# A fixed order for a kernel's first loads, and four weight copies moved from the opening into the half products

## The chip, the cores and the metric

The kernel runs on one core of one Trainium2 chip. The metric is the device time of one execution in microseconds; the median of the runs shown is compared. A core has a matrix engine (TensorE, here PE, with its weight loads as PEld), VectorE (DVE), ScalarE (ACT), GpSimd (POOL), and SyncE (SP), which here only issues transfers. Transfers are issued on the queue of SP, ACT or POOL and carried out by 16 DMA engines that all of them share.

## The reference

One inference step of a one-layer hybrid encoder in float32: 1024 prompt frames and 64 sample frames (1088 in all), model width 1024.

```
xn = rms_norm(x, g_pre)
z  = xn @ w_in                 # one projection, columns cut into
                               # xa, ga | q, k, v, gb | fl (16 columns) | ma, mb
ua = causal_conv(xa, width 4);  ya = rg_lru(ua) * silu(ga)
logf = log_sigmoid(fl + b_f)    # per head and frame
yb = softmax(q k / 8 + sum of logf between key and query, causal) v * silu(gb)
mix = (sigmoid(ma) * (ya @ w_branch[0]) + sigmoid(mb) * (yb @ w_branch[1])) @ w_o
h  = x + rms_norm(mix, g_post)
y  = h + rms_norm(sigmoid(h @ w_ple_gate) * (p @ w_ple_proj), g_ple)
```

Returned are y, the keys k, the values v, logf and the last states of branch A, for prompt and sample.

## The kernel before

**Arithmetic.** A product that must be as exact as float32 is made of three passes: each operand is split into a high part (a rounded copy made by ACT, names ending in `h`) and a low part (the difference, made by DVE, names ending in `l`), and PE adds high x high, low x high and high x low.

**Stages.** (1) The opening, 0 to some 35 us: the first two blocks of 128 frames (`x_in`) are normalised, transposed and split, while the V columns of `w_in` arrive as eight weight rows of 128 x 1024 numbers (`load_wv(k)`, k = 0 to 7, 512 KB each) and are split into `wvh` and `wvl`. Rows 0 to 2 and 5 to 7 share three buffers `wv_raw`, so row 5 can be loaded when row 0 is split, and so on; rows 3 and 4 lie in the two halves of `w_raw`. PE takes up each row for both blocks as soon as it is split (`rows(b, [k], VC)`, 6 matmuls of 346 columns each); the last 348 columns hold 16 for the forget logits too, which come from the small load `wf_raw` (128 x 8 pieces of 64 bytes). (2) The V projection of the other blocks to about 101 us, then two panels of a gate. (3) The half products: twelve passes of `seven` (from about 152 to 415 us), each of which gives two 128-column panels of k, q or a gate from seven products of half size. A pass has its raw weights loaded two passes ahead (`load_pair`, alternately into `w_raw` and `wraw`) and split one pass ahead. Keys are turned (`tpk`) and copied by ACT to a staging tile (`st`, two buffers, or `kst`, one), from which SP's queue stores them into the output (`keys_out`). `tpk`, `cum_p` and `ct` share one PSUM tag with two buffers. (4) Attention, the recurrence of branch A, the branch projections, the output projection with `w_o`, and the last normalisations.

**The copies of `w_o`.** `copy_weights(n)` copies one 512 x 512 quarter of `w_o` (1 MB) inside DRAM into `d_w`, laid out so that the output projection, after 1000 us, can load it in one piece. In the source its four calls stand in the recurrence of branch A.

**What sets the order.** PE's order is the written one; ACT and DVE keep the written order in marked stretches (`manual_schedule`), the opening among them. Everything else is placed by a scheduler, which keeps an instruction at its written place only where it is passed through `tc.keep_in_program_order`. SP executes its transfers in the order that the scheduler gives: an issue that has to wait holds up all that follow. Each transfer reports to one of eight completion counters (`DMAHW0` to `DMAHW7`), given out in turn over SP's and ACT's queues together; a transfer whose counter was last used by one that hasn't landed is not issued until that one has, and the issuing engine stands meanwhile.

Of the kernel before, what the change touches and what calls it, by code (L numbers as in the profile page):

```python
# [13 lines left out]
P = 128  # L14
D = 1024
KT = D // P
# [5 lines left out]
NH = 16  # L22
# [5 lines left out]
C_XA, C_GA, C_Q, C_K, C_V, C_GB, C_FL, C_MA, C_MB = (  # L28
    0, 1024, 2048, 3072, 4096, 5120, 6144, 6160, 7184)
# [36 lines left out]
def hybrid_step(tc, a, o):  # L66
    nc = tc.nc
    PSUM = bass.MemoryType.PSUM
    act, dve, pool, pe, sp = nc.scalar, nc.vector, nc.gpsimd, nc.tensor, nc.sync
# [8 lines left out]
    def f(ap):  # L78
        return ap.bitcast(F32)

    def copy_act(out, in_, scale=1.0):
        return act.activation(out=out, in_=in_, func=AF.Copy, scale=scale)  # L82

    def sub(eng, out, in0, in1):
        return eng.tensor_tensor(out=out, in0=in0, in1=in1, op=ALU.subtract)  # L85
# [16 lines left out]
    NW = D // 2  # L102
    d_w = dram.tile([4, P, 4 * NW], F32, name="d_w")

    def copy_weights(n):

        i, j = n // 2, n % 2
        sp.dma_start(d_w[n].rearrange("p (k n) -> p k n", k=4),
                     a["w_o"][i * NW:(i + 1) * NW, j * NW:(j + 1) * NW].rearrange("(k p) n -> p k n", p=P))


    cst = sb("cst")
# [87 lines left out]
    def run(steps):  # L200
        for _ in steps:
            pass

    def chunk(steps):
        for _ in range(KT):
            next(steps)

    w_in = a["w_in"]
# [11 lines left out]
    def panels(src):  # L220
        return [src[..., i * P:(i + 1) * P] for i in range(2)]
# [99 lines left out]
    lp = flp.tile([P, NH], F32, name="lp")  # L321
    bf = p1.tile([P, NH], F32, name="bf")
# [4 lines left out]
    wf_raw = p1.tile([P, KT, NH], F32, name="wf_raw")  # L327
    xsl = p1.tile([P, KT, P], F32R, name="xsl")
    p1x = sb("p1x")
    g_pre = p1x.tile([P, D], F32, name="g_pre")  # L330
# [4 lines left out]
    def load_x(b):  # L335
        src, n, _ = x_src[b]
        t = p1x.tile([P, D], F32, name="x_in", tag="x_in", bufs=2)
        sp.dma_start(t[:n, :], src)
        x_in.append(t)

    raws = {}

    def load_wv(k):
        if k in (3, 4):
            raw = raw_half[k - 3]
        else:
            raw = p1x.tile([P, D], F32, name="wv_raw", tag="wv_raw", bufs=3)
        sp.dma_start(raw[:, :], w_in[k * P:(k + 1) * P, C_V:C_V + D])
        raws[k] = raw

    def split_wv(k):
        raw = raws.pop(k)
        copy_act(wvh[:, k, :D], raw[:, :])
        sub(dve, wvl[:, k, :D], raw[:, :], f(wvh[:, k, :D]))
# [67 lines left out]
    def turn_diag(b):  # L422
        x, dg = x_in[b], turned[b]
        turned[b] = [p1t.tile([P, 4, P], F32, name="tp", tag="tp") for _ in range(2)]
        for k in range(KT):
            pe.matmul(turned[b][k // 4][:, k % 4, :], x[:, k * P:(k + 1) * P], dg[:, :], start=True, stop=True)

    def x_hi(b, ks):
        for k in ks:
            copy_act(xs[k][0][:, b * P:(b + 1) * P], turned[b][k // 4][:, k % 4, :], scale=gT[:, k:k + 1])  # L430
# [8 lines left out]
    gT = p1.tile([P, KT], F32, name="gT")  # L439
    load_x(0)  # L440
    act.dma_start(g8[:, :], a["g_pre"].rearrange("(k p) -> k p", p=P))
    load_wv(0)
    load_x(1)
    for k in range(1, KT):
        load_wv(k)
        if k == 4:
            sp.dma_start(wf_raw[:, :, :], w_in[:, C_FL:C_FL + NH].rearrange("(k p) n -> p k n", p=P))
    wake = p1t.tile([P, 512], F32, name="wake", tag="tp")
    g_p = mm.tile([P, 512], F32, name="g_p", tag="acc")
    for i in range(WAKE):  # L450
# [4 lines left out]
    def weights(k, c):  # L455
        c0, w = VCH[c]
        return wvh[:, k, c0:c0 + w], wvl[:, k, c0:c0 + w]
# [6 lines left out]
    def rows(b, ks, cs=(0, 1, 2)):  # L464
        for k in ks:
            xh, xl = (t[:, b * P:(b + 1) * P] for t in xs[k])
            for p in (0, 2, 1):
                for c in cs:
                    w = VCH[c][1]
                    wh, wl = weights(k, c)  # L470
                    pe.matmul(pair[b][c][:, :w], xl if p == 2 else xh, wl if p == 1 else wh,  # L471
                              start=(k == 0 and p == 0), stop=(k == KT - 1 and p == 1))
# [6 lines left out]
    turn_diag(0)  # L479
    second = rstd_diag(1)  # L480
    split_wv(0)
    next(second)
    x_hi(0, [0])
    x_lo(0, [0])
# [2 lines left out]
    rows(0, [0], VC)  # L487
    run(second)
    split_wv(1)
    rows(0, [1], VC)  # L490
    turn_diag(1)
    for ks in (range(2, 4), range(4, KT)):
        x_hi(0, ks)
        x_lo(0, ks)
    split_wv(2)
    x_hi(1, (0, 1))
    x_lo(1, (0, 1))
    rows(0, [2], VC)
    rows(1, (0, 1), VC)
    x_hi(1, range(2, KT))  # L500
    x_lo(1, range(2, KT))
    sp.dma_start(g_pre[:, :], a["g_pre"].partition_broadcast(P))
    load_x(2)
    load_x(3)
    act.dma_start(bf[:, :], a["b_f"].partition_broadcast(P))
    sp.dma_start(lp[:, :], a["cache_logf"])

    vec = p1.tile([96, P], F32, name="vec")
    at = 0
    for name in ("conv_w", "conv_b", "b_rg_a", "b_rg_x", "a_param", "state_h", "state_conv"):  # L510
        n = a[name].shape[0]
        sp.dma_start(vec[at:at + n, :], a[name])
        at += n
    V_CW, V_CB, V_BA, V_BX, V_AP, V_H0, V_HIST = 0, 32, 40, 48, 56, 64, 72
    pool.memset(fl[:, NBLK, :], 0.0)
# [66 lines left out]
    for b in range(2, NBLK + 1):  # L582
        _, n, t0 = x_src[b]
# [50 lines left out]
    def load_pair(i):  # L634
        raw = sp_.tile([P, KT, 2 * P], F32, name="wraw", tag="wraw", bufs=1)[:, :, :] if i % 2 else raw_pair
        src = quads[i][0]
        for dst, s in zip([raw] if len(src) == 1 else panels(raw), src):
            load_panel(dst, s)
        return panels(raw)

    def split_pair(i, raws_, got):

        a1, a2 = raws_
        a11, a12, a21, a22 = a1[:, :4, :], a1[:, 4:, :], a2[:, :4, :], a2[:, 4:, :]

# [24 lines left out]
        split(sp_, ("s4",), [s4], 1)  # L670
        yield
# [239 lines left out]
    for i in range(len(quads)):  # L911
        nxt, w_nxt = None, {}
        last = i + 1 == len(quads)
        if not last:
            if i + 2 < len(quads):
                pairs.append(load_pair(i + 2))
            nxt = split_pair(i + 1, pairs[i + 1], w_nxt)
        else:
            held_back[0] = False
            look_ahead()  # L920
        seven(i, w, nxt, last)
        w = w_nxt
# [323 lines left out]
    for u, (h, q2) in enumerate(units):  # L1246
        p = h // 2
# [85 lines left out]
    while s_q or t_q or v_q:  # L1333
# [156 lines left out]
    def state(k):  # L1490
        state_in(k)
        scan(k)
# [61 lines left out]
    split_u(0)  # L1554
    run(xa)
    for k in range(0, KT - 2, 2):
        for n in range(k, min(k + 2, 4)):
            copy_weights(n)
        ga = own_gate(k)
        if k == 0:  # L1560
            chunk(ga)
        gate(k)
        convolve(k + 1)
        mix_u(k)
        if k:
            early_gate(k - 1)
        if k:
            split_y(k - 2)
            chunk(ga)
        split_u(k + 1)  # L1570
        chunk(ga)
        if k:
            state(k - 1)
            output(k - 1)
        run(ga)
        own_gate(k + 1)
        xa = recur_in(k + 2)
# [99 lines left out]
    for of in range(KT):  # L1677
# [16 lines left out]
        if of == 2:  # L1694
# [4 lines left out]
            at = 0  # L1699
# [368 lines left out]
    for k in range(2):  # L2068
        raw = p7.tile([P, D], F32, name="ple")
# [67 lines left out]
    n = x_src[b][1]  # L2137
# [68 lines left out]
```

## Time and profile before

| | us |
|---|---|
| median of 3 runs | 1464.6 |
| lowest, highest | 1464.26, 1467.74 |
| the profiled execution, its time | 1467.15 |
| the profiled execution, its span | 1465.4 |
| PE busy in the span | 1436.0 |
| granted TensorE clock, mean | 0.994 |

The span runs from the first to the last instruction of the one execution that was profiled; 1.75 us of its time lie around it. PE stands still for 29.4 us in the span, and for 2.24 us of that at one place in the opening. In a row of the timeline stand the start, the length, the engine (a name ending in q is the engine's issue of a transfer), the line, the operation, what it writes and reads, the count, and in brackets how long the engine had stood before it and on whom it had waited. A table of stretches gives for each engine its busy time and number of instructions, then the granted clock (1.00 is full speed), the mean share in which the 16 DMA engines were busy, and GB/s.

### The profile page before, as it was taken

The numbers are of one execution on the slowest core, as the hardware profiler recorded it, in microseconds if no ns is written. First come the engines' busy times: TensorE is split into PE (matmuls) and PEld (weight loads), VectorE is DVE, ScalarE is ACT, GpSimd is POOL, SyncE is SP. The second block draws the span as 40 slices with busy tenths as digits, with TensorE's granted clock in tenths as the row PEclk, the third lists the DMA queues.
The fourth block names the chain that finished last, engine by engine and source line by source line (L and its number), as shares of the span: only waits on it lengthen the run. The fifth ranks groups of instructions, "written<-read, shape, count | busy, mean of one in ns | idle before, by whom it ended". The sixth has DMA issues, their size and how long they took to land.

```text
span 1465.4 us, 25652 instructions
## 1 busy us (share of the span) xinstructions
PE 1436.0 (98%) x9653; PEld 1394.7 (95%) x9653; DVE 893.7 (61%) x1631; ACT 717.1 (49%) x1353; POOL 299.1 (20%) x385
## 2 busy tenths in 40 slices
PE   8999999999999999999999999999999999999997
PEld 8999999999999999999899989999999999879997
DVE  5464866564325666666466555898755574778534
ACT  4423444442215566666456556777444232554633
POOL 0013324323123332333233210221023000000001
PEclk9999999999999999999999999999999999999999
DMA  8457456754276565646545344454278774224111
GB/s 285 143 119 109 130 163 189 181 178 127 78 210 157 120 148 139 141 112 139 118 129 128 61 108 70 86 101 84 99 235 273 257 218 152 100 86 171 43 43 44
DMA packets 149304, 200.64 MB, mean 137 GB/s; under 512 B 24212, under 2 KB 115836, under 8 KB 148156
## 3 DMA queue, kind: packets, MB, share of 16 engines
q1 hardware_dynamic: 129772, 167.06, 44.2%
q10 hardware_dynamic: 17680, 25.64, 5.1%
q0 software_dynamic: 1728, 6.29, 2.3%
q8 instruction: 76, 1.25, 0.4%
q14 instruction: 48, 0.39, 0.1%
HBM read 131.04 MB, written 65.80 MB: 134 GB/s over the span
## 4 chain that ended last, share of the span: by engine, by line
PE 84%; DVE 7%; ACT 4%; DMA 3%; issue 2%; SPq 0%; POOL 0%; ACTq 0%; DVEq 0%; POOLq 0%
PE quad L805 17%; PE acc L170 12%; PE acc L172 12%; PE acc L171 12%; PE q L1853 5%; PE tp L1147 4%; PE pv L1175 2%; PE s L1125 2%; PE s L1126 2%; PE pv L1177 2%; PE vacc L170 1%; PE vacc L171 1%; PE vacc L172 1%; PE vacc L471 1%; PE q L1978 1%
## 5 line engine op out<-in xcount | busy, mean ns | idle before, releaser
L170 PE MATMUL acc<-xh,wh 128*128 128x364 f32 (+1 forms) x768 | 253.2, 330 | 1.3 <-ACT st L82 1.2
L171 PE MATMUL acc<-xl,wh 128*128 128x364 f32 (+1 forms) x768 | 252.0, 328 | 0.0
L172 PE MATMUL acc<-xh,wl 128*128 128x364 f32 (+1 forms) x768 | 251.8, 328 | 0.0
L170 PEld LDWEIGHTS acc<-xh,wh 128*128 128x128 f32 x768 | 144.9, 189 | 2.6 <-ACT st L82 1.9
L171 PEld LDWEIGHTS acc<-xl,wh 128*128 128x128 f32 x768 | 144.7, 188 | 0.5
L172 PEld LDWEIGHTS acc<-xh,wl 128*128 128x128 f32 x768 | 144.5, 188 | 0.0
L1105 DVE CUSTOM_DVE_ANT_0 s<-s,mask 128x1024 f32<-128x1024 f32 (+7 forms) x128 | 95.5, 767 | 26.8 <-PE s L1126 26.7
L85 DVE TENSOR_TENSOR wl<-w_raw,wh 128x1024 fp32r<-128x1024 f32 (+1 forms) x54 | 62.6, 1160 | 67.3 <-ACT wh L82 66.3
L1110 POOL TENSOR_SCALAR pb<-pb,sm 128x896 f32<-128x896 f32 (+1 forms) x64 | 61.8, 966 | 196.2 <-DVE sm L1109 178.2
L82 ACT ACTIVATE wh<-w_raw 128x1024 fp32r<-128x1024 f32 (+1 forms) x66 | 64.3, 976 | 65.6 <-PE quad L805 27.3
L85 DVE TENSOR_TENSOR tl<-tp,th 128x512 fp32r<-128x512 f32 x96 | 65.7, 688 | 35.6 <-ACT th L82 35.6
L805 PE MATMUL quad<-xh,wh 128*128 128x272 f32 x384 | 80.7, 291 | 0.0
L805 PE MATMUL quad<-xl,wh 128*128 128x272 f32 x384 | 79.5, 288 | 0.0
L805 PE MATMUL quad<-xh,wl 128*128 128x272 f32 x384 | 79.4, 288 | 0.0
L82 ACT ACTIVATE th<-tp 128x512 fp32r<-128x512 f32 x96 | 56.9, 596 | 40.6 <-PE tp L1147 33.4
L1107 ACT ACTIVATE pb<-s,nm 128x896 f32<-128x896 f32 (+1 forms) x64 | 61.1, 954 | 30.0 <-DVE nm L1105 27.7
L1125 PE MATMUL s<-k,q 128*128 128x256 f32 (+1 forms) x192 | 67.1, 353 | 0.2 <-ACT pb L1107 0.2
L1147 PE MATMUL tp<-ident,pb 128*128 128x128 f32 x416 | 63.9, 274 | 1.2 <-DVE diag0l L85 0.7
L1126 PE MATMUL s<-k,q 68*128 68x256 f32 (+1 forms) x192 | 65.0, 350 | 0.0
L171 PE MATMUL acc<-ybl,wh 128*128 128x364 f32 (+1 forms) x192 | 62.9, 328 | 0.0
L172 PE MATMUL acc<-ybh,wl 128*128 128x364 f32 (+1 forms) x192 | 62.8, 327 | 0.0
L170 PE MATMUL acc<-ybh,wh 128*128 128x364 f32 (+1 forms) x192 | 62.7, 326 | 0.0
(705 smaller groups left out, 4151.8 us busy)
## 6 DMA issues: line engine op xcount, KB each, us to landing
w_raw<-in_w_in SPq DMA_DIRECT2D x56, 256.0 KB
q<-d_q SPq DMA_DIRECT2D x48, 256.0 KB
k<-d_k SPq DMA_DIRECT2D x48, 256.0 KB
w_raw<-in_w_in SPq DMA_DIRECT2D x64, 128.0 KB
w_raw<-in_w_branch SPq DMA_DIRECT2D x32, 256.0 KB
wl<-w_raw POOLq DMA_DIRECT2D x12, 512.0 KB, 4.6
wraw<-in_w_in SPq DMA_DIRECT2D x20, 256.0 KB
d_k<-oh ACTq DMA_DIRECT2D x16, 272.0 KB
```

What stands on the lines that cost most here:

```text
L82: return act.activation(out=out, in_=in_, func=AF.Copy, scale=scale)
L85: return eng.tensor_tensor(out=out, in0=in0, in1=in1, op=ALU.subtract)
L170: pe.matmul(out, ah, bh, start=start, stop=False)
L171: pe.matmul(out, ah, bl, start=False, stop=False)
L172: pe.matmul(out, al, bh, start=False, stop=stop)
L805: pe.matmul(acc[:, c, :CW], l[:, k, :], r[:, k, c * CW:(c + 1) * CW], start=(first and k == 0 and p == 0), stop=(k == 3 and p == 2), skip_ ...
L1105: at = book("D", now[0] + HOP_PE, per(D_MAX, n), lambda: dve.tensor_tensor_reduce(out=s[:, :n], in0=s[:, :n], in1=m, scale=-1.0, scalar=-N ...
L1110: return free, book("G", at, per(G_NORM, n), lambda: pool.tensor_scalar(out=pr[:, :n], in0=pr[:, :n], scalar1=sm, scalar2=1.0, op0=ALU.mul ...
L1125: pe.matmul(s[:, c0:c0 + w], t["q1"][:, q0:q0 + P], t["k1"][:, c0:c0 + w], start=True, stop=False)
L1126: pe.matmul(s[:, c0:c0 + w], t["q2"][:HD + 4, q0:q0 + P], t["k2"][:HD + 4, c0:c0 + w], start=False, stop=True)
L1147: pe.transpose(tp[:, o0 + i * P:o0 + (i + 1) * P], pr[par][:, kb * P:(kb + 1) * P], ident[:, :])
L1853: pe.matmul(acc, l[:, k, :], r[:, k, :], start=(first and k == 0 and i == 0), stop=(k == 3 and i == 2), skip_group_check=not first)
```

## The change

All loads of the opening are fixed in the order in which they are written (`fetch`), and that order is: the two blocks of `x` and rows 0 to 4; rows 5, 6 and 7 after the splits of rows 0, 1 and 2; then the third block of `x`, `wf_raw`, `g_pre`, the fourth block, and the small vectors. `b_f`'s load, which ACT issues, stands right behind the load of `g8`. The four copies of `w_o` are taken out of branch A and written, fixed in place, into passes 0 to 3 of the half products, each behind that pass's `load_pair`.

```diff
     def copy_weights(n):
         i, j = n // 2, n % 2
-        sp.dma_start(d_w[n]..., a["w_o"][...])
+        tc.keep_in_program_order(sp.dma_start(d_w[n]..., a["w_o"][...]))
...
     def load_x(b):
...
-        sp.dma_start(t[:n, :], src)
+        fetch(t[:n, :], src)
...
+    def fetch(dst, src):
+        tc.keep_in_program_order(sp.dma_start(dst, src))
...
     def load_wv(k):
...
-        sp.dma_start(raw[:, :], w_in[k * P:(k + 1) * P, C_V:C_V + D])
+        fetch(raw[:, :], w_in[k * P:(k + 1) * P, C_V:C_V + D])
...
     load_x(0)
     act.dma_start(g8[:, :], a["g_pre"].rearrange("(k p) -> k p", p=P))
+    act.dma_start(bf[:, :], a["b_f"].partition_broadcast(P))
     load_wv(0)
     load_x(1)
-    for k in range(1, KT):
+    for k in range(1, 5):
         load_wv(k)
-        if k == 4:
-            sp.dma_start(wf_raw[:, :, :], ...)
...
     split_wv(0)
+    load_wv(5)
...
     split_wv(1)
+    load_wv(6)
...
     split_wv(2)
+    load_wv(7)
...
-    sp.dma_start(g_pre[:, :], a["g_pre"].partition_broadcast(P))
     load_x(2)
+    fetch(wf_raw[:, :, :], ...)
+    fetch(g_pre[:, :], a["g_pre"].partition_broadcast(P))
     load_x(3)
-    act.dma_start(bf[:, :], a["b_f"].partition_broadcast(P))
-    sp.dma_start(lp[:, :], a["cache_logf"])
+    fetch(lp[:, :], a["cache_logf"])
...
     for name in ("conv_w", "conv_b", "b_rg_a", "b_rg_x", "a_param", "state_h", "state_conv"):
-        sp.dma_start(vec[at:at + n, :], a[name])
+        fetch(vec[at:at + n, :], a[name])
...
             if i + 2 < len(quads):
                 pairs.append(load_pair(i + 2))
+            if i < 4:
+                copy_weights(i)
             nxt = split_pair(i + 1, pairs[i + 1], w_nxt)
...
     for k in range(0, KT - 2, 2):
-        for n in range(k, min(k + 2, 4)):
-            copy_weights(n)
         ga = own_gate(k)
```

SP's queue in the opening, before, from the fourth and fifth weight rows on, with the counters that each issue waits for (`L338` loads `x`, `L348` a weight row, `L447` is `wf_raw`, `L512` the small vectors):

```order
L348 DMA w_raw<-in_w_in 128x1024 x2
L447 DMA wf_raw<-in_w_in 128x8x16 [waits DMAHW0_49]
L502 DMA g_pre<-in_g_pre 128x1024 [waits DMAHW1_49]
L506 DMA lp<-in_cache_logf 128x16 [waits DMAHW2_49]
L512 DMA vec<-in_conv_w 32x128 [waits DMAHW3_49]
L348 DMA wv_raw<-in_w_in 128x1024 [waits DMAHW4_49,DVE_49]
L338 DMA x_in<-in_x_prompt 128x1024 [waits DMAHW5_49,PE_49]
L512 DMA vec<-in_conv_b 8x128 [waits DMAHW6_49]
L512 DMA vec<-in_b_rg_a 8x128 [waits DMAHW7_49]
L512 DMA vec<-in_b_rg_x 8x128 [waits DMAHW0_49]
L348 DMA wv_raw<-in_w_in 128x1024 [waits DMAHW1_49,DVE_49]
```

The same stretch in the changed kernel, where `L345` is the line of `fetch`:

```order
L345 DMA w_raw<-in_w_in 128x1024 [waits DMAHW0_49]
L345 DMA wv_raw<-in_w_in 128x1024 [waits DMAHW2_49,DMAHW1_49,DVE_49]
L345 DMA wv_raw<-in_w_in 128x1024 [waits DMAHW5_49,DVE_49]
L345 DMA wv_raw<-in_w_in 128x1024 [waits DMAHW6_49,DMAHW3_49,DVE_49]
L345 DMA x_in<-in_x_prompt 128x1024 [waits DMAHW4_49,PE_49]
L345 DMA wf_raw<-in_w_in 128x8x16
L345 DMA g_pre<-in_g_pre 128x1024
L345 DMA x_in<-in_x_prompt 128x1024 [waits DMAHW7_49,PE_49]
L345 DMA lp<-in_cache_logf 128x16 [waits DMAHW0_49]
L345 DMA vec<-in_conv_w 32x128 [waits DMAHW1_49]
```

Rows 5 to 7 now stand ahead of all small loads, and `wf_raw` behind the third block of `x`. The counter that the load of `conv_b` waited for, 6, is that of the fourth weight row, the seventh transfer of the two queues if one counts from 0 with `g8`.

ACT's stream behind the last splits of the second block of `x`, before:

```order
L82 ACTIVATE xh_110<-tp,gT 128x128 [waits PE_49]
L82 ACTIVATE xh_110<-tp,gT 128x128 x3
L505 DMA bf<-in_b_f 128x16 [waits DMAHW6_49]
L82 ACTIVATE wvh<-w_raw 128x1024
L82 ACTIVATE wvh<-w_raw 128x1024 [waits DMAHW7_49]
```

In the changed kernel the load of `b_f` stands as ACT's fourth instruction, behind the copy to `warm` and ahead of the first square of `x`, and waits for nothing, and here the split of the fourth row follows at once:

```order
L82 ACTIVATE xh_110<-tp,gT 128x128 [waits PE_49]
L82 ACTIVATE xh_110<-tp,gT 128x128 x3
L82 ACTIVATE wvh<-w_raw 128x1024 [waits DMAHW7_49]
L82 ACTIVATE wvh<-w_raw 128x1024 [waits DMAHW0_49]
```

SP's queue in the second half product of the changed kernel; before, the same rows stood there without the `d_w`:

```order
L255 DMA wraw<-in_w_in 128x2x256 [waits DMAHW6_49]
L855 DMA d_k<-kl 128x544 [waits DMAHW7_49,DVE_49]
L255 DMA wraw<-in_w_in 128x2x256 [waits DMAHW0_49]
L108 DMA d_w<-in_w_o 512x1x512 [waits DMAHW1_49]
L830 DMA out_k_prompt<-kst 128x256 [waits DMAHW2_49,Activation_49]
L830 DMA out_k_prompt<-st 128x256 [waits DMAHW3_49,Activation_49]
L830 DMA out_k_prompt<-st 32x256 [waits DMAHW4_49,Activation_49]
```

The copy stands between the last piece of the pass's raw weights and the stores of the keys. The fourth copy stands in the same way behind the last two pieces of `wraw` and ahead of three stores of keys; the first and the third follow a piece of `w_raw` and are followed by `d_k<-kl` and `d_q<-ko`. Beside this, ACT's stream differs in one place: in the fourth half product two copies `st<-tpk` stand behind `cr<-ct` and `ko<-quad` and no longer ahead of them. The streams of PE, DVE and POOL hold the same instructions in the same order.

More of the change, by code (lines that the diff above doesn't have):

```diff
@@ L107, in copy_weights @@
         i, j = n // 2, n % 2
-        sp.dma_start(d_w[n].rearrange("p (k n) -> p k n", k=4),
-                     a["w_o"][i * NW:(i + 1) * NW, j * NW:(j + 1) * NW].rearrange("(k p) n -> p k n", p=P))
+        tc.keep_in_program_order(sp.dma_start(
+            d_w[n].rearrange("p (k n) -> p k n", k=4),
+            a["w_o"][i * NW:(i + 1) * NW, j * NW:(j + 1) * NW].rearrange("(k p) n -> p k n", p=P)))
     cst = sb("cst")
@@ L441, in hybrid_step @@
     act.dma_start(g8[:, :], a["g_pre"].rearrange("(k p) -> k p", p=P))
+    act.dma_start(bf[:, :], a["b_f"].partition_broadcast(P))
     load_wv(0)
     load_x(1)
-    for k in range(1, KT):
+    for k in range(1, 5):
         load_wv(k)
-        if k == 4:
-            sp.dma_start(wf_raw[:, :, :], w_in[:, C_FL:C_FL + NH].rearrange("(k p) n -> p k n", p=P))
     wake = p1t.tile([P, 512], F32, name="wake", tag="tp")
@@ L501, in hybrid_step @@
     x_lo(1, range(2, KT))
-    sp.dma_start(g_pre[:, :], a["g_pre"].partition_broadcast(P))
     load_x(2)
+    fetch(wf_raw[:, :, :], w_in[:, C_FL:C_FL + NH].rearrange("(k p) n -> p k n", p=P))
+    fetch(g_pre[:, :], a["g_pre"].partition_broadcast(P))
     load_x(3)
-    act.dma_start(bf[:, :], a["b_f"].partition_broadcast(P))
-    sp.dma_start(lp[:, :], a["cache_logf"])
+    fetch(lp[:, :], a["cache_logf"])
     vec = p1.tile([96, P], F32, name="vec")
```

## The prediction

> **What bounds the kernel now.** First the page's busy table: TensorE (PE) is busy 98% of the span, so the time is PE's work plus the 29 us in which it stands still, and a change of loads can only move those stalls, or the clock at which PE runs.
>
> ```profile
> span 1465.4 us, 25652 instructions
> PE 1436.0 (98%) x9653; PEld 1394.7 (95%) x9653; DVE 893.7 (61%) x1631; ACT 717.1 (49%) x1353; POOL 299.1 (20%) x385
> ```
>
> Then the table of stretches through the opening (columns: length, busy time of PE, PEld, DVE, ACT and POOL, granted clock, DMA share, GB/s). PE stands from 22 to 24 and runs at half clock from 25 to 28.
>
> ```profile
> 22.00:24.00 2.00, 0.14 (x1) 0.00 (x0) 0.00 (x0) 0.73 (x1) 0.00 (x0) 1.00 0.84 252
> 25.00:28.00 3.00, 2.98 (x11) 2.54 (x10) 3.00 (x4) 2.38 (x4) 0.00 (x0) 0.50 0.80 186
> ```
>
> Then the timeline, to see who is late. ScalarE (ACT) ends the sixth `xh` at 18.18 + 1.66 = 19.84 and should split the fourth weight row. The next thing in its stream, though, is the issue of `b_f`'s load, and that waits for a completion counter last used by the load of `conv_b`. That one was issued at 13.68 behind 512 KB of `x` and landed only at 22.8; the split follows at 23.27 and PE at 24.38.
>
> ```profile
> 13.68 2.38 SPq L512 DMA_DIRECT2D vec<-in_conv_b  x1
> 18.18 1.66 ACT L82 ACTIVATE xh<-tp,gT 128x128 fp32r<-128x128 f32 x6 [0.68 <-DVE xl L435]
> 22.85 0.38 ACTq L505 DMA_DIRECT2D bf<-in_b_f  x1
> 23.27 2.00 ACT L82 ACTIVATE wvh<-w_raw 128x1024 fp32r<-128x1024 f32 x2 [3.44 <-DMA vec<-in_conv_b]
> 24.38 0.67 PE L471 MATMUL vacc<-wvh,xh 128*128 128x346 f32 x2 [2.24 <-ACT wvh L82]
> ```
>
> **The change, part by part. First the opening.** With `b_f` issued at the top (ACT is idle there until `x` lands at 4.59), nothing stands between 19.84 and the split. The fourth row had landed by 13.68: `conv_b` could be issued then only because that row had freed the same counter.
>
> ```profile
> 0.81 0.40 SPq L338 DMA_DIRECT2D x_in<-in_x_prompt  x1
> 4.59 0.63 ACT L408 ACTIVATE xn<-x_in 128x512 f32<-128x512 f32 x1 [1.65 <-DMA x_in<-in_x_prompt]
> 9.93 0.37 ACT L82 ACTIVATE xh<-tp,gT 128x128 fp32r<-128x128 f32 x1 [0.46 <-PE tp L426]
> 15.66 1.21 DVE L85 TENSOR_TENSOR wvl<-wv_raw,wvh 128x1024 fp32r<-128x1024 f32 x1
> 19.11 0.32 PE L471 MATMUL vacc<-wvh,xh 128*128 128x346 f32 x1
> 21.82 0.32 PE L471 MATMUL acc<-wvl,xh 128*128 128x346 f32 x1
> 27.09 0.29 ACT L82 ACTIVATE wvh<-wf_raw 128x128 fp32r<-128x128 f32 x1
> 31.98 0.32 PE L471 MATMUL vacc<-wvh,xh 128*128 128x348 f32 x1
> 8.00:14.00 6.00, 4.66 (x34) 4.08 (x34) 4.09 (x12) 4.32 (x12) 0.00 (x0) 1.00 0.94 335
> 18.12 0.27 SPq L512 DMA_DIRECT2D vec<-in_b_rg_x  x1
> SPq L512 <- DMA wf_raw<-in_w_in: 1.7, 1, 1.7
> ```
>
> At full clock these matmuls follow each other every (21.82 - 19.11) / 17 = 0.159 us. The steps of rows 3 to 5 are 2 blocks x 3 rows x 6 = 36 matmuls, 5.74 us. They fill 21.98 to 31.98 now, 10.0 us. If every split is in time they end at 27.72, a gain of 4.26 us: 2.4 us of standing, 1.9 us of half clock and a short wait for `wvl`. In time they are: a row costs ACT 1.0 us (2.00 for two) and DVE 1.2 us, PE uses one up in 1.9 us, and the fourth row, begun at 19.84, is done by ACT at 20.9 and by DVE at 22.1, before PE's third pair of matmuls at 22.6. The sixth to eighth rows are issued as soon as their buffers come free, the last at 16.9 (15.66 + 1.21, the end of the third split), not behind the vectors, and at 335 GB/s each takes 1.6 us.
>
> What is late next is `wf_raw`, now behind all rows and `x`. The old trace has it landing at 18.1, at most 4.4 us after the fourth row at 13.68, with the fifth row between. Now the last row and `x` come ahead of it, 16.9 + 3.8 (the first load of `x`, from 0.81 to 4.59) + 1.6 = 22.3 at the latest, so `wf_raw` lands at 23 to 26.7, and ACT and DVE need 0.6 us for it before PE wants it at 27.7. I take no cost; 1 us if it takes 6 us rather than 4.4. `g_pre` and the vectors are wanted after 30. `b_f`'s small packets, now among the first loads, can delay the first weight row by some tenths, which ACT's wait of 0.46 us for PE before the first `xh` swallows. Bounds for the opening: -4.3 to -2.5; taken -4.2.
>
> **The four copies of `w_o`.** They leave a stretch where only they move data.
>
> ```profile
> 23.52 2.96 SPq L108 DMA_DIRECT2D d_w<-in_w_o  x3
> 29.00:33.00 4.00, 4.00 (x27) 4.00 (x26) 3.24 (x10) 1.72 (x4) 0.00 (x0) 1.00 1.05 398
> d_w<-in_w_o SPq DMA_DIRECT2D x4, 1024.0 KB
> ```
>
> One copy holds the queue for 1.049 MB / 398 GB/s = 2.6 us. PE is busy all through that stretch, so taking them away gains nothing; what counts is what they are now ahead of on SP's queue. Copies 1 and 3 follow `w_raw` pieces near 156 and 200.5, and the DMA engines then fall idle, which hides them:
>
> ```profile
> 151.94 4.14 SPq L254 DMA_DIRECT2D w_raw<-in_w_in  x4
> 200.06 0.44 SPq L254 DMA_DIRECT2D w_raw<-in_w_in  x1
> 160.00:162.00 2.00, 1.27 (x11) 1.04 (x9) 2.00 (x2) 0.00 (x0) 1.30 (x2) 1.00 0.00 0
> 206.00:208.00 2.00, 2.00 (x18) 2.00 (x18) 0.00 (x0) 0.22 (x1) 0.00 (x0) 1.00 0.00 0
> ```
>
> Copies 2 and 4 come straight ahead of stores of K, whose staging tiles ACT needs back. Copy 2:
>
> ```profile
> 181.98 0.47 SPq L824 DMA_DIRECT2D out_k_prompt<-kst  x1
> 186.97 0.38 ACT L82 ACTIVATE kst<-tpk 128x256 f32<-128x256 f32 x1 [1.53 <-DMA out_k_prompt<-kst]
> 190.66 0.37 ACT L82 ACTIVATE kst<-tpk 96x256 f32<-96x256 f32 x1
> 191.56 0.39 PE L732 MATMUL cum_p<-lf,tri 128*128 128x128 f32 x2
> ```
>
> The store issued at 181.98 lands at 186.9, and ACT has waited 1.53 us for it already. Behind a copy it lands 2.6 us later. ACT has no gap to give back from 186.97 to 190.66 but its own queue, so the last `kst` ends at 193.6 instead of 191.03. It empties the PSUM buffer that `cum_p` takes (tag `acc`, two buffers, `tpk` and `cum_p` in turn). PE wants it at 191.56: slack 0.53, stall 2.6 - 0.5 = 2.1 us. Copy 4:
>
> ```profile
> 225.98 1.77 SPq L254 DMA_DIRECT2D wraw<-in_w_in  x2
> 227.85 0.89 SPq L824 DMA_DIRECT2D out_k_prompt<-st  x2
> 231.74 0.71 ACT L82 ACTIVATE st<-tpk 128x256 f32<-128x256 f32 x2 [0.51 <-DMA out_k_prompt<-st]
> 233.79 0.60 PE L816 MATMUL tpk<-ident,ko 128*128 128x128 f32 x4
> ```
>
> The two `st` would end at 232.45 + 2.6 = 235.05, and the `tpk` at 233.79 needs the buffer they empty: stall 1.25 us. The one swap on ACT puts `cr` and `ko` ahead of these `st`, so the wait no longer holds the bank of the product. Together 3.35 us; bounds 0 (the store overtakes the copy, or the DMA engines' slack takes it) to 8.4 (rival below).
>
> **The clock after a stall** is the third term. Idle 2.4 us at 22 gave half clock, and so did 1.85 us here; 1.19 us did not:
>
> ```profile
> 1068.53 0.43 PE L172 MATMUL acc<-yah,wl 128*128 128x364 f32 x1 [1.85 <-DVE wl L85]
> 1069.00:1073.00 4.00, 4.00 (x16) 4.00 (x15) 2.65 (x4) 0.75 (x1) 0.00 (x0) 0.57 0.67 214
> 1019.72 0.43 PE L170 MATMUL acc<-xh,wh 128*128 128x364 f32 x1 [1.19 <-ACT st L82]
> 1019.00:1023.00 4.00, 3.28 (x20) 3.28 (x21) 3.93 (x5) 1.83 (x5) 0.76 (x3) 1.00 0.79 161
> ```
>
> A drop costs (1 - 0.57) x 4.0 = 1.7 us. The 1.25 us stall I take as harmless; the 2.1 us one as 0 to 1.7, nearer the upper end: 1.2. The Trainium skill speaks against this term: "TensorE: Matmul & The Clock Gate", section "Why this matters for your kernels", allows idle gaps up to about 3 us; by it the sum would be 1.2 us lower. The rows above differ from the page, and I go by them.
>
> **Sum.** -4.2 + 2.1 + 1.25 + 1.2 = +0.35 us. The profiled execution took 1467.15 (span 1465.4 and 1.75 around it) and so would become 1467.5; the runs shown have their median 2.55 lower, at 1464.6, so the forecast is 1464.9.
>
> **Rivals.** (1) *The copies are hidden*: the gain of the opening stands alone. For it: PE's slack in the half products may be larger than two tile reuses show, as most waits there are ACT's for PE. Against: ACT waits for these very stores already. 1464.6 - 4.2 = 1460.4. (2) *Slower: the copies hold the stores longer.* If a copy beside the 1 KB rows of `wraw` moves at the 204 GB/s below instead of 398, it delays the store by 5.1 us: stalls 4.6 + 3.8 with half clock after both, 3.4, less 4.2 is +7.6, 1472.2. It is slower by more than 4.4 us from a delay of 3.5 us on (two delays less 1.85 of slack, plus 3.4, less 4.2); at 3.7 us it gives 1469.4. For it: the DMA engines are well used there; against: they are not full.
>
> ```profile
> 181.00:187.00 6.00, 6.00 (x50) 5.97 (x50) 1.95 (x2) 1.83 (x4) 0.00 (x0) 1.00 0.72 204
> ```
>
> (3) *`wf_raw` takes the removed wait's place*: the gain shrinks by 1 to 2 us, with the copies' cost 1466.5. That the scheduler keeps the old order is excluded by the listed order.
>
> **Chances.** Forecast 0.50 (own range 1462.5 to 1467), rival 1 0.27, rival 2 0.15, rival 3 0.08. A measurement tells 0.3%, 4.4 us, from no change. Rival 1 lies just inside that bound and passes it in some 4 of 10 cases: faster 0.27 x 0.4 + 0.03 = 0.14. Slower: two thirds of rival 2 and 0.03 of the tails, 0.13. Same 0.73. Range 1460.0 to 1468.8: rival 1 and the lower half of rival 2's cases, the others whole.
>
> **What would show it.** Right: no ACT wait before the split of the fourth row, PE at full clock from 18 on, the first 348-column matmul near 27.7; `kst` waiting some 4 us for its store near 183 to 186, and PE idle about 2 us before `cum_p` and 1 us before the `tpk` of the fourth half product. Wrong: no PE idle at these two places (rival 1), idle over 3 us (rival 2), or ACT waiting for `wf_raw` with PE idle behind it (rival 3).

## The result: 0.35% slower, and where the time went

The changed kernel takes 1472.9 us in the median (1467.5 to 1476.9), the kernel before, run beside it, 1467.45 (1464.3 to 1468.8). The ratio is 1.0035 with a 95% interval of 1.0024 to 1.0046, about 5.1 us more. The forecast was 1464.9, no change. Of the 8.0 us between, 2.9 are the base: three runs had put the kernel before at 1464.6, more runs put it at 1467.45, which the profiled execution's 1467.15 had already said. The two medians differ by 5.45 us, where the sum had 0.35; that is the other 5.1.

The busy table of the changed kernel:

```profile
span 1471.7 us, 25655 instructions
PE 1434.6 (97%) x9653; PEld 1393.2 (95%) x9653; DVE 893.9 (61%) x1631; ACT 716.7 (49%) x1353; POOL 295.1 (20%) x385
```

The span grew by 6.3 us and PE's busy time fell by 1.4, so in the net the loss is standing still. (A stretch at half clock counts as busy; such stretches came and went.) PE's waits by whom it waited for (total us, times, longest):

```profile
PE acc L171 <- ACT st L82: 4.0, 2, 2.9
PE tpk L822 <- ACT st L82: 3.4, 2, 3.0
PE cum_p L738 <- issue: 3.0, 1, 3.0
```

The wait of 2.2 us for `wvh` is gone; three waits of about 3 us have come. Two stand where the prediction put them, the first was in none of its cases. In order of time:

**The opening** went as forecast. Timeline and stretches of the changed kernel:

```profile
17.39 1.66 ACT L82 ACTIVATE xh<-tp,gT 128x128 fp32r<-128x128 f32 x6 [0.68 <-DVE xl L439]
18.91 2.04 ACT L82 ACTIVATE wvh<-w_raw 128x1024 fp32r<-128x1024 f32 x2
26.51 0.31 ACT L82 ACTIVATE wvh<-wf_raw 128x128 fp32r<-128x128 f32 x1 [3.66 <-DMA wf_raw<-in_w_in]
27.50 0.32 PE L474 MATMUL vacc<-wvh,xh 128*128 128x348 f32 x1
```

```profile
20.00:25.00 5.00, 5.00 (x34) 5.00 (x33) 4.75 (x5) 2.85 (x3) 0.00 (x0) 1.00 0.62 213
25.00:30.00 5.00, 5.00 (x33) 5.00 (x32) 2.12 (x7) 2.50 (x5) 0.00 (x0) 1.00 0.34 124
```

The split of the fourth row follows the last `xh` with no wait, PE runs through at full clock, and the first matmul of 348 columns starts at 27.50 in place of 31.98: 4.48 us earlier. `wf_raw` came late, as forecast, and just early enough: ACT waited 3.66 us for it, PE did not.

**The gate panels near 140 us** took 2.7 us back, in this execution. Timeline, first of the changed kernel, then of the kernel before:

```profile
130.22 1.30 POOL L85 TENSOR_TENSOR s<-s,w_raw 128x512 f32<-128x512 f32 x1 [4.51 <-issue]
130.32 4.64 DVE L85 TENSOR_TENSOR t3l<-rc,t3h 128x1088 fp32r<-128x1088 f32 x2 [2.29 <-ACT t3h L82]
135.00 3.40 DVE L572 TENSOR_TENSOR rc<-xh,xl 128x2176 f32<-128x2176 f32 x1
140.88 1.11 ACT L82 ACTIVATE t4h<-rc 128x1088 fp32r<-128x1088 f32 x1 [6.72 <-DVE rc L85]
141.90 0.45 ACT L82 ACTIVATE st<-acc 128x360 f32<-128x360 f32 x1
142.41 0.43 PE L171 MATMUL acc<-xh,wh 128*128 128x364 f32 x1 [2.85 <-ACT st L82]
```

```profile
134.17 2.49 DVE L85 TENSOR_TENSOR t3l<-rc,t3h 128x1088 fp32r<-128x1088 f32 x2 [3.14 <-ACT t3h L82]
136.70 2.42 DVE L566 TENSOR_TENSOR rc<-xh,xl 128x2176 f32<-128x2176 f32 x1
136.77 3.50 POOL L85 TENSOR_TENSOR s<-s,w_raw 128x512 f32<-128x512 f32 x1 [6.61 <-DVE t3l L85]
```

Before, POOL's sums began behind `t3l`; here they began 0.1 us ahead of it. VectorE's two `t3l` took 4.64 us in place of 2.49 and the next sum 3.40 in place of 2.42; the third took 2.42 in place of 3.39, as POOL was done by then, so the chain was 2.1 us longer. ACT's `t4h` waits for that chain, the copy `st` that frees PE's bank stands behind `t4h` on ACT, and PE stood 2.85 us. The Trainium skill, "GPSIMD Engine Reference", section "Key points", says that GpSimd shares its SBUF interfaces with VectorE and contends with VectorE instructions that read two inputs from SBUF; these rows agree.

**The copies** 2 and 4 did what the forecast said, at about twice its price. Timeline of the changed kernel:

```profile
180.04 0.59 SPq L108 DMA_DIRECT2D d_w<-in_w_o  x1
180.72 0.65 SPq L830 DMA_DIRECT2D out_k_prompt<-kst  x1
189.35 0.39 ACT L82 ACTIVATE kst<-tpk 128x256 f32<-128x256 f32 x1 [5.62 <-DMA out_k_prompt<-kst]
193.03 0.37 ACT L82 ACTIVATE kst<-tpk 96x256 f32<-96x256 f32 x1
193.50 0.77 PE L738 MATMUL cum_p<-lf,tri 128*128 128x128 f32 x2 [2.98 <-issue]
240.72 0.73 ACT L82 ACTIVATE st<-tpk 128x256 f32<-128x256 f32 x2 [4.12 <-DMA out_k_prompt<-st]
241.51 0.65 PE L822 MATMUL tpk<-ident,ko 128*128 128x128 f32 x4 [3.04 <-ACT st L82]
```

ACT now waits 5.62 us for the store of `kst`, not 1.53. The last `kst` of the pass ends at 193.40, and at 193.50 `cum_p` starts; the profile writes "issue" there; by the order of the rows it is the PSUM buffer that came free. How slow a copy is where it now stands, and what the clock did behind the two stalls:

```profile
182.00:184.00 2.00, 2.00 (x19) 2.00 (x18) 0.23 (x1) 1.18 (x2) 0.00 (x0) 1.00 0.94 138
184.00:186.00 2.00, 2.00 (x18) 2.00 (x17) 0.99 (x1) 0.00 (x0) 0.00 (x0) 1.00 0.88 255
186.00:188.00 2.00, 2.00 (x19) 2.00 (x18) 0.00 (x0) 0.00 (x0) 0.00 (x0) 1.00 0.92 341
```

```profile
192.50:199.30 6.80, 5.80 (x26) 5.72 (x27) 4.20 (x15) 1.82 (x5) 0.00 (x0) 0.50 0.84 210
241.00:245.00 4.00, 3.49 (x28) 3.50 (x29) 2.56 (x4) 2.69 (x7) 0.12 (x1) 1.00 0.69 223
```

From the first to the last piece of copy 2, by the trace's records of single transfers, 6.3 us pass, not 2.6: while it starts up (182 to 184) the DMA engines are counted busy 0.94 and move 138 GB/s in all. A piece of 2 KB took 0.28 to 0.52 us on average there, and 0.084 us from 186 us on. Around `cum_p` the clock stood at half for 6.8 us, in 5.8 of which PE worked; the stall of 3.04 us before `tpk` was followed by no half clock.

**One gain by chance.** Near 1070 us the wait of 1.85 us that had cost the kernel before a stretch at half clock recurs almost the same, and is followed by none:

```profile
1076.45 0.43 PE L173 MATMUL acc<-yah,wl 128*128 128x364 f32 x1 [1.82 <-DVE wl L85]
1076.00:1080.00 4.00, 3.55 (x21) 3.55 (x22) 2.42 (x4) 1.70 (x2) 0.00 (x0) 1.00 0.53 134
```

PE's stream holds the same matmuls in the same order in both kernels, so the start of each can be subtracted from its old one. The difference, and its steps:

| place | step, us | total, us |
|---|---|---|
| opening, to 28 us | -4.4 | -4.4 |
| wait for `st`, 142 us | +2.7 | -1.7 |
| `tpk` and `cum_p` of pass 1, 190 us | +3.6 | +1.9 |
| half clock behind it | +2.6 | +4.5 |
| `tpk` of pass 3, 241 us (and 0.3 to 295 us) | +3.5 | +8.0 |
| no half clock at 1070 us | -1.6 | +6.4 |

The two profiled executions therefore differ by 6.4 us past 1074 us, by 6.2 at the last matmul and by 6.3 in the span.

### The profile page after: what moved, and what is told of

Same layout as the page of the kernel before. It is cut to its first block, busy times and chain, and to the rows that moved or that the text cites. A ratio compares the mean times of both kernels' runs of the same rounds, so it can differ in the third digit from the quotient of the medians.

```text
span 1471.7 us, 25655 instructions
## 1 busy us (share of the span) xinstructions
PE 1434.6 (97%) x9653; PEld 1393.2 (95%) x9653; DVE 893.9 (61%) x1631; ACT 716.7 (49%) x1353; POOL 295.1 (20%) x385
## 3 DMA queue, kind: packets, MB, share of 16 engines
q8 instruction: 76, 1.25, 0.4%
## 4 chain that ended last, share of the span: by engine, by line
PE 79%; DVE 9%; DMA 4%; ACT 4%; issue 2%; SPq 0%; ACTq 0%; POOL 0%; DVEq 0%
PE quad L811 15%; PE acc L171 12%; PE acc L173 12%; PE acc L172 12%; PE q L1859 5%; PE tp L1155 4%; PE pv L1183 3%; PE pv L1185 2%; PE s L1133 2%; PE s L1134 2%; PE vacc L171 1%; PE vacc L172 1%; PE vacc L173 1%; PE vacc L474 1%; DMA out_v_prompt<-v_sb 1%
```

## The experiments

Theory: the opening's gain is real and comes from `b_f`'s load alone; copies 2 and 4, since they stand ahead of the stores of keys, cost it all and more. Rival: the new order of loads has shifted the completion counters, and the stores are late through these. All ratios below are to the kernel before, with 95% intervals; 0.001 is 1.47 us. Steps "at a matmul" are differences of the start of the same matmul, from the traces.

One thing is wrong in two of the expectations (the copies alone, and `b_f` with the last block first): they put a wait of 1.2 us for `st` near 143 us in the kernel before. It stands at 1019.7 us; near 143 PE did not wait at all.

### The copies back in the opening

```diff
+    for n in range(2):          # behind the small vectors
+        copy_weights(n)
...
     load_x(4)
+    for n in range(2, 4):
+        copy_weights(n)
...
-            if i < 4:
-                copy_weights(i)
```

> The changed kernel, with the four copies of w_o issued in the opening again: two behind the small vectors, two behind the fifth block of x. Everything else of the change stays. Theory (copies 2 and 4 hold up the stores of keys): PE idles less than 0.5 us before cum_p of the second half product and before the tpk of the fourth, the half clock behind cum_p is gone, together 3.2 + 2.6 + 3.2 = 9 us less than the changed kernel; the opening keeps its 4.4 us, and the wait of 2.9 us for the copy st near 140 us, which I put down to the opening, stays. So about 1.7 us below the kernel before, ratio 0.999. Rival (the new order of the first loads has shifted the completion counters, and the stores come late through these): both stalls stay at 3 us without the copies, and the ratio stays near 1.003.

Measured: 0.9982 (0.9973 to 0.9990). Neither stall of the half products is there, nor half clock. But the opening's gain, 5.1 us at 30 us, shrank by 2.3 us at one place. Timeline:

```profile
32.14 1.29 SPq L108 DMA_DIRECT2D d_w<-in_w_o  x2
43.91 11.16 SPq L345 DMA_DIRECT2D x_in<-in_x_prompt  x2
54.14 1.29 PE L394 MATMUL tp<-ident,xn 128*128 128x128 f32 x8 [1.89 <-DVE xn L378]
```

Copies 3 and 4 now stood ahead of the sixth block of `x`, and PE waited 1.89 us for it. The wait for `st` near 140 us, expected to stay at 2.9 us, was 1.51. The theory on the stores holds; the copies cost wherever something that is wanted soon stands behind them.

### The copies alone

The kernel before with the moved copies, fixed in place, and nothing else of the change.

```diff
+            if i < 4:
+                copy_weights(i)
...
-        for n in range(k, min(k + 2, 4)):
-            copy_weights(n)
```

> The kernel before, with only the copies of w_o moved into passes 0 to 3 of the half products; the opening is the old one. Theory: both stalls of some 3 us appear, with half clock behind the first, about 9 us above the kernel before, ratio 1.006; near 143 us PE waits 1.2 us as before. Rival (counters shifted by the opening): no new stall, ratio 1.000. If taking the copies out of the opening is worth something by itself there, the ratio lies between.

Measured: 1.0057 (1.0040 to 1.0075), 8.4 us more. Timeline and stretches:

```profile
194.51 0.77 PE L733 MATMUL cum_p<-lf,tri 128*128 128x128 f32 x2 [2.98 <-issue]
242.60 1.11 PE L817 MATMUL tpk<-ident,ko 128*128 128x128 f32 x4 [2.88 <-ACT st L82]
```

```profile
194.00:200.80 6.80, 6.29 (x29) 6.21 (x30) 3.70 (x14) 1.34 (x4) 0.00 (x0) 0.50 0.85 214
241.80:248.60 6.80, 6.00 (x27) 5.97 (x28) 2.56 (x4) 2.97 (x7) 0.52 (x2) 0.50 0.73 196
```

The same two stalls without the new opening: the rival on counters falls. Here the clock stood at half for 6.8 us at both, so this profiled execution lost more than that of the changed kernel.

### The load of `b_f` alone

```diff
     act.dma_start(g8[:, :], ...)
+    act.dma_start(bf[:, :], ...)
...
     load_x(3)
-    act.dma_start(bf[:, :], ...)
```

> The kernel before, with only the load of b_f moved ahead; the order of the other loads and the copies are as before. Theory of the prediction (ACT's wait at b_f's issue is the whole gain of the opening): the stall of 2.2 us at 24 us and the half clock behind it are gone, PE 4.4 us earlier at 60 us. If the stall near 140 us comes with the earlier start alone, 2.7 us are given back there and the ratio is 0.999; if not, it is 0.997. Rival (the order of the weight rows is needed too): the stall is shorter by less than 2 us, since wf_raw, g_pre and the vectors still stand ahead of rows 5 to 7.

Measured: 0.9957 (0.9944 to 0.9970), 6.3 us less. ACT's row:

```profile
18.73 2.04 ACT L82 ACTIVATE wvh<-w_raw 128x1024 fp32r<-128x1024 f32 x2
```

No wait, no half clock, PE 5.4 us earlier at 28 us, of which about 1 us is a half clock near 15 us that this execution did not have. No wait for `st` near 140 us. One moved line gives all that the opening has to give.

### The copies in even passes

```diff
-            if i < 4:
-                copy_weights(i)
+            if i in (0, 2, 4, 6):
+                copy_weights(i // 2)
```

> The changed kernel, with the copies in passes 0, 2, 4 and 6 of the half products in place of 0 to 3, so that none stands ahead of stores of keys on SP's queue. Theory: no new stall before cum_p and before the tpk; as e1 about 9 us less than the changed kernel, ratio 0.999 to the kernel before, although each copy may still take 6 us and more. Rival (any copy in the half products costs): the stalls move to other passes, and the ratio stays above 1.002.

Measured: 0.9963 (0.9949 to 0.9977), 5.4 us less than before and 0.72%, 10.6 us, less than the changed kernel. Its opening is that of the changed kernel, its copies still take 4.8 to 7.8 us each, and PE does not stand before `cum_p`:

```profile
186.31 0.39 PE L738 MATMUL cum_p<-lf,tri 128*128 128x128 f32 x2
```

So what a copy costs here is set by what waits behind it on the queue, not by how long it takes.

### Copy 2 alone ahead of the stores

The even passes, with copy 2 in pass 1.

```diff
-            if i in (0, 2, 4, 6):
-                copy_weights(i // 2)
+            if i in (0, 1, 4, 6):
+                copy_weights((0, 1, 4, 6).index(i))
```

> The kernel of the even passes, with copy 2 back in pass 1, straight ahead of the stores of keys; copies 1, 3 and 4 in passes 0, 4 and 6. Theory: PE idles 3.2 us before cum_p and loses 2.6 us more to half clock behind it, none before the tpk of pass 3: 5.8 us over the even passes, about 1467 us. Rival (the cost needs both copies, or lies in copies 1 and 3): within 1 us of the even passes.

Measured: 1.0013 (1.0002 to 1.0025), 0.50%, 7.3 us, above the even passes; 5.8 were expected. ACT and PE:

```profile
185.75 0.38 ACT L82 ACTIVATE kst<-tpk 128x256 f32<-128x256 f32 x1 [5.62 <-DMA out_k_prompt<-kst]
189.88 0.46 PE L738 MATMUL cum_p<-lf,tri 128*128 128x128 f32 x2 [2.98 <-issue]
```

No stall before the `tpk` of pass 3. The stall of 2.98 us is the same in four kernels (this one, the changed kernel, the copies alone, and the changed kernel with the last block first), while the `tpk` ahead of it waited 0.31 to 0.67 us: once the late `kst` has freed PE's `tpk`, the last `kst` is still behind `ko`, `oh` and two `wh` on ACT, 4.05 us in the changed kernel (189.35 to 193.40). ACT's own queue, which the prediction counted only as "no gap to give back", sets the length. By difference copy 4 costs 0.22%, 3.2 us; the two intervals nearly touch, so this figure is rough. ACT's swapped order in pass 3 comes with copy 4 (here, as in the even passes, it is the old one), so the two were not tested apart; ACT's row names the store, with 4.12 us.

### Half copies and double copies

Each copy cut in two, one half in each of passes 0 to 7; then copies 1 and 2 together in pass 1, 3 and 4 in pass 3.

```diff
+            if i < 8:
+                copy_weights(i // 2, slice(2 * (i % 2), 2 * (i % 2) + 2))
```

> The changed kernel, with each copy cut into two of 512 KB, one in each of passes 0 to 7; so half a copy stands ahead of the stores in passes 1, 3, 5 and 7. In the changed kernel the copy to kst of pass 1 came 4.1 us late and PE idled 3.2 us. Theory A (a copy has a start-up and then moves at some 400 GB/s): it comes 2.8 us late, PE idles about 1.9 us before cum_p. Theory B (a copy beside other loads moves at some 170 GB/s all through): 2.0 us late, PE idles 1.1 us or less, without half clock. Time by A about 1467 us, by B about 1463; the even passes cost nothing.

```diff
+            if i in (1, 3):
+                copy_weights(i - 1)
+                copy_weights(i)
```

> The changed kernel, with copies 1 and 2 together in pass 1 and 3 and 4 together in pass 3, so that 2 MB stand ahead of the stores. ACT's order differs in a few places beside it. Theory A (start-up, then 400 GB/s): the two copies take 6.2 + 2.6 = 9 us, kst comes 6.7 us late, PE idles some 5.8 us before cum_p. Theory B (170 GB/s): the two take 12.4 us, kst comes 8 us or more late, PE idles over 7 us. Time by A about 1480, by B 1485 us.

Measured: halves 1.0005 (0.9994 to 1.0017), doubles 1.0056 (1.0033 to 1.0080). ACT and PE in pass 1, halves:

```profile
183.12 0.39 ACT L82 ACTIVATE kst<-tpk 128x256 f32<-128x256 f32 x1 [2.88 <-DMA out_k_prompt<-kst]
187.27 0.46 PE L738 MATMUL cum_p<-lf,tri 128*128 128x128 f32 x2 [0.75 <-issue]
```

The same `kst` with two copies ahead, PE behind it, and a stretch from the middle of the copies:

```profile
189.70 0.38 ACT L82 ACTIVATE kst<-tpk 128x256 f32<-128x256 f32 x1 [7.51 <-DMA out_k_prompt<-kst]
190.93 0.63 PE L822 MATMUL tpk<-ident,ko 128*64 128x128 f32 x2 [3.88 <-ACT st L82]
192.46 0.77 PE L738 MATMUL cum_p<-lf,tri 128*128 128x128 f32 x2 [0.90 <-issue]
184.00:186.00 2.00, 2.00 (x19) 2.00 (x17) 0.35 (x1) 0.00 (x0) 0.00 (x0) 1.00 1.06 403
```

From the first piece to the last, half a copy takes 3.4 us, one 6.1, two 9.1 (records of single transfers). From the issue of the copy to the start of `kst`, which is when the store ahead of it has landed, 6.7, 9.5 and 13.5 us pass; in the kernel before, from the store's own issue, 5.0 (181.98 to 186.97). Theory A fits what the copies themselves take: a second copy behind the first adds 3.0 us at up to 403 GB/s. Neither fits the store's delay: A was right for the halves' `kst` (2.8 us late against the even passes' 180.33), B for the stall behind it (0.75 us), and with two copies `kst` is 8.6 us late (9.4 less the 0.8 by which this execution was behind), where A said 6.7 and B 8 or more. With 5.4 us for one copy (185.75 against 180.33), a copy holds up this store by some 4 to 5.5 us per MB. With two copies PE did not stand 5.8 or 7 us before `cum_p`, but 3.88 before the `tpk` and 0.90 before `cum_p`; ACT's order differs there. The times test the theories less well than these rows: the halves took 1467.9 us (A 1467, B 1463), but they also lost 0.7, 0.9 and 1.3 us in passes 3, 5 and 6, the last where no cost was expected; the doubles took 1474.9 us, less than either theory (1480 and 1485).

### Copy 2 on ACT's queue

```diff
             sp.dma_start(dst, st[:n, :2 * P])
             t0 += n
+            if n_st[0] == 5:
+                copy_weights(1, act)
```

> As the kernel with copy 2 alone ahead of the stores of keys, but copy 2 is issued by ACT on its own queue, at nearly the same time, straight behind the two copies to st of pass 1. Theory A (the store waits because it stands behind the copy in SP's queue): the next copy to kst is not late any more, PE idles under 0.5 us before cum_p, time as the even passes, 1461 us. Theory B (the 16 DMA engines are shared, and the copy takes their time from any store): kst is 2 us late or more, PE idles 1 to 3 us, time 1463 to 1468 us. ACT's order differs in two places (the split of w_raw and the copy ko) beside it.

Measured: 0.9977 (0.9967 to 0.9986), between the even passes (0.9963) and the same copy on SP's queue (1.0013). SP, ACT and PE:

```profile
177.35 0.50 SPq L830 DMA_DIRECT2D out_k_prompt<-kst  x1
178.87 0.69 ACTq L108 DMA_DIRECT2D d_w<-in_w_o  x1
181.80 0.39 ACT L82 ACTIVATE kst<-tpk 128x256 f32<-128x256 f32 x1 [1.56 <-DMA out_k_prompt<-kst]
188.09 0.38 ACT L82 ACTIVATE kst<-tpk 96x256 f32<-96x256 f32 x1 [2.52 <-DMA out_k_prompt<-kst]
188.57 0.46 PE L738 MATMUL cum_p<-lf,tri 128*128 128x128 f32 x2 [1.89 <-issue]
```

Both theories are half right. The next `kst` comes 4 us earlier than with the copy on SP's queue (181.80 for 185.75), so the order of copy and store is most of the cost; but the store issued while the copy moved (at 182.21) kept the `kst` of 188.09 waiting, and PE stands 1.89 us. One thing is not told apart: the copy was issued here 1.5 us behind the store of 177.35, and on SP's queue 0.7 us ahead of it, so its place in time changed with the queue. The Trainium skill, "DMA: Bandwidth & Descriptors", section "Issuing engines are not separate DMA queues", says that transfers of all issuing engines run on the same 16 DMA engines and interleave, so that a second queue saves little but issue time. The remaining 1.89 us agree with the sharing; the 0.36%, 5.3 us, between the two kernels say that here the move, with the later place in time that came with it, was worth more than issue time: the store no longer stood behind the whole copy.

### The last block of the panel copied out first

```diff
-    split_half(rc, T4, 0)
     run(steps)
+    split_half(rc, T4, 0)
     split_half(rc, T4, 1)
```

Three kernels have this edit: the even passes, the changed kernel, and `b_f` alone.

> The kernel of the even passes, and in the gate panels near 140 us ACT copies the panel's last block out of PSUM ahead of the first half of t4h instead of behind it. Theory (the wait of 2.9 us for st there comes about only where POOL's sums start ahead of VectorE's t3l and slow VectorE down, since t4h, and st behind it, wait for VectorE): PE has no wait for st there in any order of POOL and VectorE, the runs spread less than the 5.4 us of the even passes, and the median is that of its quick runs, 1461 us, ratio 0.996. Rival (the wait has another cause, a transfer): the spread stays.

> The changed kernel, copies in passes 0 to 3 as there, with the panel's last block copied out of PSUM ahead of t4h in the gate panels near 140 us. Theory (part of the changed kernel's time is PE's wait of 2.9 us for st near 140 us, which comes about in the executions in which POOL's sums start ahead of VectorE's t3l): no wait for st there in whichever order POOL and VectorE start, the stalls before cum_p and tpk stay at 3 us each, and the median falls by 0 to 2.7 us below the changed kernel, to a ratio of 1.002 to 1.0035. Rival (the wait has another cause): it stays.

> The kernel before, with b_f's load ahead and the panel's last block copied out ahead of t4h; loads and copies as before. If PE's wait for st near 143 us (1.2 us before, none with b_f alone) is a matter of chance from execution to execution, this is as b_f alone or better by up to 1 us, ratio 0.995 to 0.9965, with a spread under 3 us.

Measured: even passes 0.9966 (0.9954 to 0.9979, unedited 0.9963), changed kernel 1.0043 (1.0029 to 1.0057, unedited 1.0035), `b_f` alone 0.9957 (0.9944 to 0.9969, unedited 0.9957). No median moved. In the even passes:

```profile
132.03 2.93 POOL L85 TENSOR_TENSOR s<-s,w_raw 128x512 f32<-128x512 f32 x1 [7.18 <-DVE t3l L85]
134.74 0.47 ACT L82 ACTIVATE st<-acc 128x360 f32<-128x360 f32 x1 [2.00 <-PE acc L173]
```

ACT copies the block out as soon as PE is done with it, so the wait cannot arise there. But in none of these three profiles did POOL start ahead of `t3l`; so the theory's condition was not met, and that POOL's early start makes the wait is read from profiles, not shown by an intervention. A second profile agrees in part. With the copies back in the opening POOL began at 134.23, ahead of the sum behind `t3l`, and that sum took 3.42 us again; PE stood 1.51 us:

```profile
134.23 1.30 POOL L85 TENSOR_TENSOR s<-s,w_raw 128x512 f32<-128x512 f32 x1 [6.79 <-DMA out_v_sample<-v_sb]
134.39 3.42 DVE L576 TENSOR_TENSOR rc<-xh,xl 128x2176 f32<-128x2176 f32 x1
```

In the other twelve profiles POOL began behind that sum's start, and it took 2.42 or 2.43 us. What is shown is that the wait is not what makes the changed kernel slow: without the possibility of it the median is the same. The runs spread less (1460.2 to 1463.1 for 1460.8 to 1466.2; changed kernel 1472.2 to 1475.2 for 1467.5 to 1476.9); that is weak evidence, as spreads are.

### `b_f` and the even passes, without the fixed order

The kernel before with these two edits (the copies fixed in place):

```diff
     act.dma_start(g8[:, :], ...)
+    act.dma_start(bf[:, :], ...)
...
-    act.dma_start(bf[:, :], ...)
...
+            if i in (0, 2, 4, 6):
+                copy_weights(i // 2)
...
-        for n in range(k, min(k + 2, 4)):
-            copy_weights(n)
```

> The kernel before, with b_f's load ahead and the copies in passes 0, 2, 4 and 6; the other loads of the opening are as before, not in the fixed order. Theory (the fixed order is worth nothing beside b_f, and copies in even passes cost nothing): as the kernel of the even passes and as b_f alone, ratio 0.996. Rival (the copies' absence from the opening, or the fixed order, is worth something of its own): more than 1.5 us off the even passes.

Measured: 0.9973 (0.9961 to 0.9984). Against 0.9963 with the fixed order and 0.9957 with the copies in the opening the intervals overlap. The distance from the even passes is 1.5 us, just at the rival's bound: whether the fixed order of the loads and the copies' absence from the opening are worth a little is not settled; the difference is smaller than the intervals.

## Why the prediction was wrong, point by point

- **The opening, -4.2: right.** Measured -4.4 in the profile, and the mechanism row by row as said: no ACT wait, full clock, 27.50 for the forecast 27.7. In time it is worth 0.37 to 0.43% (even passes, `b_f` alone), 5.4 to 6.3 us, some of it in a half clock near 15 us that comes and goes.
- **`wf_raw`, taken as no cost: right.** Split at 26.51, inside the forecast 23 to 26.7 for its landing; rival 3 is out.
- **Copies 1 and 3 hidden: right**, by the even passes, where four such copies cost nothing.
- **"One copy holds the queue for 1.049 MB / 398 GB/s = 2.6 us": this step failed.** The 398 GB/s was read in the middle of a train of copies that had the DMA engines nearly to themselves; in that same train the first 1 MB, beside loads at its start, had taken 4.6 us (from 25.81 to 30.37), the second 2.7. A single copy among other transfers starts slowly, 138 GB/s in its first 2 us; copy 2 took 6.3 us in the changed kernel (6.1 to 7.7 in four kernels) and copy 4 5.7 (3.6 to 5.7 in three). The last `kst` came 4.1 us late (193.40, where 191.03 less the 1.7 us that the kernel was ahead gives 189.3) in place of 2.6, the delay at `cum_p` was 3.6 in place of 2.1, at the `tpk` of pass 3 3.3 in place of 1.25. The profile shown had a nearer row: copy 2 would stand among loads that moved at 204 GB/s, as rival 2 said. The Trainium skill's "DMA: Bandwidth & Descriptors", section "Bandwidth", gives 6.15 us for a load of 1 MB on another kind of queue; copy 2 took 6.3 here, and with that figure the sum would have been on the slower side.
- **The clock, +1.2 of 0 to 1.7: undersized.** It cost 2.6 us at one stall and nothing at the other; in the copies alone the clock stood at half for 6.8 us at both. The upper bound assumed one stretch of 3.4 us; a stall near 3 us can give two. The Trainium skill, "TensorE: Matmul & The Clock Gate", section "Why this matters for your kernels", allows gaps up to about 3 us; the rows above differ, as 2.98 us was followed by half clock.
- **The sum.** Copies and clock came to 9.7 us in the profile where the forecast had 4.55; that accounts for 5.1 of the 6.0 us by which this profile missed the sum. The rest is the two steps named last below, +1.1 together, less 0.2 of the opening. In time they cost 0.72%, 10.6 us.
- **Rival 2 was what happened**, in kind and nearly in size: it priced a delay of 5.1 us at +7.6 us and set the turn at 3.5 us; the delay was 4.1 and 4.5 us (240.72, where 231.74 plus the 4.5 that the kernel was behind gives 236.2). It had been given 0.15 since the DMA engines "are not full"; while copy 2 moved (182 to 188 us) they were counted 0.88 to 0.94 busy.
- **Not in any case:** POOL's sums overtaking VectorE near 130 us, 2.7 us in this execution, and the missing half clock at 1070 us, 1.6 us the other way: two strokes of chance, bad and good. The first shows that a gain upstream can be spent where the order of two other engines varies from execution to execution.

What stays open: why a copy moves so little in its first 2 us while the DMA engines count as busy (its pieces, and those of the loads beside it, take several times as long), what POOL waits for near 130 us (the profiles name VectorE's `t3l` in some kernels and a transfer in others), and how often it starts first.

## What to carry to other kernels

Price a transfer that is moved by what stands behind it on its queue and by how long a transfer of its kind took in like company, not by the rate of an undisturbed train. Put a bulk copy where the next thing on the queue is wanted late: one moved line in the opening was worth 0.4%, and two copies in the wrong passes cost 0.7%. A kernel with `b_f`'s load ahead and everything else as before beats both kernels, at 0.9957.

## What the runs showed that was not expected

A stall's length need not follow its cause: 2.98 us before `cum_p` in four kernels, since what PE waits for is ACT's queue behind the late tile. The half clock at like stalls differs from execution to execution: none, 3.4 or 6.8 us at stalls of 2.85 to 3.04 us; 1.75 us of idleness gave it in the copies alone and 1.82 us did not in the changed kernel. The traces show what differs. Their records of the clock change in steps of 3.41 us; if each of the fourteen traces is cut into stretches of 3.41 us at these steps, then past the opening a stretch at full clock with 1.84 us or more of idle PE was always followed by half clock (27 cases), one with 1.70 us or less never, and between the two both occur. In the opening less was enough, 1.46 us in one execution. The stall of 3.04 us fell across a step, 1.79 us before it and 1.26 behind it; that of 2.98 us lay with 2.25 us in one stretch. And a sum on POOL beside a two-input sum on VectorE lengthened VectorE's from 2.49 to 4.64 us, depending on which began first.
